# Giving the gate/up weights' buffers three places of their own, 32, 96 and 160 bytes (modulo 256) behind those of the rows, and the small buffers 224

## The chip, the cores and the metric

The kernel runs on one core of one Trainium2 chip. The metric is device time in microseconds (us) of one execution, as the median of several runs. TensorE is called PE, its weight loads PEld, VectorE DVE, ScalarE ACT, GpSimd POOL, and SyncE, which issues the DMA transfers, SP.

## What is computed

Two layers of a decoder trunk over 512 positions of width 1024, in float32. A layer mixes tokens in three ways at once (spatial gating, retention, forgetting attention), projects the result back, then runs a gated MLP with a short causal convolution, and adds a gated embedding. The part that the change is about is the MLP:

```python
def conv_gated_mlp(h, w_gate, w_up, conv_w, conv_b, w_down):   # D_FF = 4096
    g = h @ w_gate                                   # 512 x 1024 by 1024 x 4096
    gp = jnp.pad(g, ((0, 0), (CONV_WIDTH - 1, 0), (0, 0)))
    conv = conv_b + gp[:, 0:S] * conv_w[0]
    for j in range(1, CONV_WIDTH):
        conv = conv + gp[:, j:j + S] * conv_w[j]
    act = jax.nn.gelu(conv, approximate=True) * (h @ w_up)
    return act @ w_down                              # 512 x 4096 by 4096 x 1024

    h = rmsnorm(x, ffn_pre_g[i])
    x = x + rmsnorm(conv_gated_mlp(h, ...), ffn_post_g[i])
    gate = jax.nn.sigmoid(rmsnorm(x, ple_pre_g[i]) @ w_ple_gate[i])
    e = p[i] @ w_ple_proj[i]
    x = x + rmsnorm(e * gate, ple_post_g[i])
```

## The kernel before

**Precision.** Each float32 operand of a large product is split into a high part in TensorE's fp32r format and the remainder: `split` (L629) lets ACT copy the high part and DVE subtract it from the source. A product of two split operands takes three matmuls (high by high, high by low, low by high; `mm3`, L786).

**Gate and up together.** The MLP (`ffn`, L1120) treats w_gate and w_up in 32 blocks of 128 columns. `gate_up` (L1137) computes both products of a block in the manner of a fast matrix multiplication: the 512 positions and the 1024 features are halved, and seven products of 128 x 512 weights with 512 x 256 rows take the place of eight. The seven sums of the rows (hb11, hb21, hh6, hd, hh7, hb22, hh4) are made once per layer. The sums of the weights are made per block: the raw weights come in a tile `graw` (1 MB, two DMAs of 512 KB), `wg` and `wu` are split from it, then DVE adds parts of it to one another in place (four additions of 128x512), then `wsa` is split from the first half and `wsb` from the second. `product` (L1132) runs 12 matmuls of 128x128 weights (stationary) by 256 columns of the rows (moving). The products in order are two of wg, two of wsa, two of wsb and one of wu, 84 matmuls, for each of 32 blocks in each of two layers: 768 matmuls per product in all. They gather in two PSUM banks, `beta` and `ag`. Between the first product of wsa and those before it ACT must copy `beta` to `gs`, since wsa's product goes on adding to the same bank. So PE waits for that copy unless it has other work.

**Down.** After `wsb` of a block come pieces of the down product of the four blocks before (`pieces`, L1209; `down`): matmuls of 512 columns into `dn`, from `act` (the split activations, stationary) and `thl` (split weights, moving). The product of wu stands between the first 22 and the last 2 of such a piece.

**What sets the order.** Nothing in this code runs directly. The class `Plan` (L51) records every operation; `issue` (L247) simulates the engines with modelled costs and emits the operations in the order of that simulation, for each engine. An operation may start in the model only when its tiles have slots. All tiles of 8 KB per partition share one tag, "b8", with 24 slots of which every one belongs to a set, `SETS`. A tile of a named kind may take a slot of its own set only; a tile without a kind (raw weights, x, the embedding's `e`, gains, sums) takes a slot of the set with most room left (`pick`, L307). The kinds are given by `b8` (L545): W for wg, wsa and wsb; X for every other tile of type fp32r, among them the rows, `act` and `thl`. The `wu` tiles are of 2 KB and lie with `gs`, `us`, `cv` and other small tiles in the pool `kp`.

**Where the buffers lie.** The pools are opened one after another (L525 to L531): the set X, a pad, the set W, then `kp`. The pad is a tile of 16 floats per partition. Since the slots are of 8192 bytes and the base of X is a multiple of 256, every X slot lies at 0 modulo 256, and every W slot and every tile of `kp` at 64.

**The start of an MLP.** Before block 0 PE computes the embedding product (`embed`, L1285): its results, two tiles `e`, are copied from PSUM by ACT and DVE and stored to DRAM through SP, and the tiles are in use until those stores have landed. The first two blocks' weights are split at the same time.

Of the kernel before, what the change touches and what calls it, by code (L numbers as in the profile page):

```python
# [28 lines left out]
F32 = mybir.dt.float32  # L29
F32R = mybir.dt.float32r  # L30
# [6 lines left out]
P = 128  # L37
# [13 lines left out]
class Plan:  # L51
# [5 lines left out]

    SETS = {"X": 18, "W": 6}  # L60

    AHEAD = {"mix": 460, "wo": 230, "wo2": 230, "emb": 185, "gu0": 720, "gu": 460, "dn": 245, "end": 770, "pg": 450, "pg2": 120}
    LOAD = 1290
# [48 lines left out]
    def sets(self, pools):  # L112

        def tile_(shape, dt, name, kind):
            key = f"t{len(self.tiles)}"

            def make():
                c, i = self.place[key]
                return pools[c].tile(shape, dt, tag=f"{c}{i}", name=name, bufs=1)
            self.tiles[key] = ["b8", sum(self.SETS.values()), [], False, make, dt]  # L120
            self.kind[key] = kind
# [125 lines left out]
    def issue(self):  # L247
# [17 lines left out]
        for t in first:  # L265
            tag, bufs = self.tiles[t][0], self.tiles[t][1]
            slots.setdefault(tag, [0.0] * bufs)
            live.setdefault(tag, np.zeros(n + 1, np.int16))[first[t]:last[t] + 1] += 1
        unused = {c: [(0.0, i) for i in range(k)] for c, k in self.SETS.items()}
        inside = {c: np.zeros(n + 1, np.int16) for c in self.SETS}  # L270
        for t, c in self.kind.items():
# [12 lines left out]
        then, kind = None, "T"  # L284
        parked = {tag: [] for tag in (*slots, *(f"b8 {k}" for k in (*self.SETS, None)))}
        taken = {}
# [20 lines left out]
        def pick(t):  # L307

            if self.kind[t] is not None:
                c, s = self.kind[t], first[t]  # L310
                return c if unused[c] and (s <= front or inside[c][front:s].max() < self.SETS[c]) else None
            room = [(self.SETS[c] - inside[c][front:last[t] + 1].max(), c) for c in self.SETS if unused[c]]
            spare, c = max(room, default=(0, None))
# [204 lines left out]
def body(ctx, tc, a, out):  # L518
    nc = tc.nc
    plan = Plan(tc)  # L520
    V, A, G, T, SY = (plan.engine(n, e) for n, e in (
        ("DVE", nc.vector), ("ACT", nc.scalar), ("POOL", nc.gpsimd), ("PE", nc.tensor), ("SP", nc.sync)))
# [2 lines left out]
    large = {}  # L525
    for i, c in enumerate(Plan.SETS):
        large[c] = ctx.enter_context(tc.tile_pool(name="b" + c, bufs=1))
        if i + 1 < len(Plan.SETS):
            pad = ctx.enter_context(tc.tile_pool(name=f"pad{i}", bufs=1)).tile([P, 16], F32, tag="pad", name="pad", bufs=1)
            nc.gpsimd.memset(pad, 0.0)  # L530
    kp = ctx.enter_context(tc.tile_pool(name="kp", bufs=1))  # L531
    wp = ctx.enter_context(tc.tile_pool(name="wp", bufs=1))
    pp = ctx.enter_context(tc.tile_pool(name="pp", bufs=8, space=bass.MemoryType.PSUM))
# [9 lines left out]
        return kpt(list(shape), dt, tag="wk", name=name, bufs=12)  # L543

    def b8(name, shape, dt=F32):  # L545
        kind = "W" if name in ("wg", "wsa", "wsb") else "X" if dt == F32R else None
        return b8t([P] + list(shape), dt, name, kind)

    def small(name, n, dt=F32, bufs=4):
# [13 lines left out]
    class Rows:  # L563
# [3 lines left out]
        def load(self, c, queue=SY):  # L567
            if self.t[c // 2] is None:
                self.t[c // 2] = b8("x", (2, D))
            queue.dma_start(out=self[c], in_=self.src[:, c, :])  # L570
# [7 lines left out]
    class Gains:  # L578
# [5 lines left out]
        def __getitem__(self, at):  # L584
            if self.t is None:
                self.t = b8("gain", (2, D))
                for i, src in enumerate(self.src):
                    if src is not None:
                        name, l = src
                        SY.dma_start(out=self.t[:, i, :], in_=a[name][l:l + 1, :].to_broadcast([P, D]))  # L590
            return self.t[at]
# [56 lines left out]
    class Plain:  # L648
# [6 lines left out]
        def __call__(self, c, x):  # L655
            if self.t is None:
                self.t = [[b8("hT", (4, S), F32R) for _ in range(2)] for _ in range(2)]
                self.rs = small("rs", NCH)
            for kh in range(2):
                cs = slice(kh * 512, kh * 512 + 512)  # L660
                h = wk("h")
                V.tensor_tensor(out=h, in0=x[:, cs], in1=self.g[:, 1, cs], op=ALU.mult)
                pv = v4(transposed(h))
                ts = slice(c * P, c * P + P)
                split(self.t[0][kh][:, :, ts], self.t[1][kh][:, :, ts], pv)
# [730 lines left out]
```

## Time and profile before

| | before |
|---|---|
| runs | 1590.88, 1589.14, 1589.31 us |
| median of the runs | 1589.31 us |
| the profiled execution | 1587.76 us |
| its span in the trace | 1585.7 us |
| PE busy | 1559.8 us (98%), 10034 matmuls |
| DVE busy | 1233.2 us (78%) |
| ACT busy | 837.2 us (53%) |
| DMA | 197.47 MB, mean 125 GB/s |

The span is that part of the profiled execution in which instructions run. Busy time is a sum over an engine's instructions. In the rows of groups, the first number after the bar is busy time and the second the mean duration of one instruction; a matmul starts before the one ahead of it has ended, so the time from start to start (called the pitch here) is shorter than a duration. In a timeline's row stand the start in the span, the duration of the whole row, the engine, the line, the instruction with output and inputs, and, in brackets, a wait ahead of it and its releaser. All recorded operations carry the line of the helper, L444, so instructions are told apart by their tiles.

### The profile page before, as it was taken

The page shows a single profiled execution, that of the slowest core. Times are in us where ns is not written, and L with a number is a line of the kernel's source. Part 1 is how long each engine was busy: PE and PEld are TensorE (multiplying, and loading weights), DVE is VectorE, ACT ScalarE, POOL GpSimd, SP SyncE. Part 2 cuts the span into 40 slices and gives each one's busy share as a digit, 9 for nine tenths or more (in the row PEclk, how much of TensorE's full clock was granted, in tenths as well). Part 3 has the DMA queues.
Part 4 walks back from the last instruction along what each step waited for, and adds up shares of the span by engine and source line. Part 5 has one row for each costly group of instructions (what it writes and reads, how often), then busy time and mean ns, then how long its engine had stood idle before and what let it go on. Part 6 is the DMA issues. An engine that isn't in the chain of part 4 may idle for free.

```text
span 1585.7 us, 25202 instructions
## 1 busy us (share of the span) xinstructions
PE 1559.8 (98%) x10034; PEld 1388.1 (88%) x10034; DVE 1233.2 (78%) x2013; ACT 837.2 (53%) x1380; POOL 91.3 (6%) x157
## 2 busy tenths in 40 slices
PE   7999998999999999999999999989999999999998
PEld 6887787999999999998888777889999999999987
DVE  6556869988878888878664658699887897898785
ACT  7324637665555555554552446477655555555453
POOL 1100020000000000002220000200000000000021
PEclk9999999999999999999999999999999999999999
DMA  8113147223323422424463023362332233234433
GB/s 316 68 55 107 61 168 265 81 80 115 125 81 103 137 80 88 153 100 180 179 250 107 28 80 116 125 252 81 108 116 97 92 123 106 83 131 134 148 141 124
DMA packets 63421, 197.47 MB, mean 125 GB/s; under 512 B 7348, under 2 KB 15164, under 8 KB 63304
## 3 DMA queue, kind: packets, MB, share of 16 engines
q1 hardware_dynamic: 63160, 195.81, 35.1%
q8 instruction: 78, 1.28, 0.3%
q14 instruction: 39, 0.32, 0.1%
q10 hardware_dynamic: 144, 0.07, 0.0%
HBM read 178.52 MB, written 17.33 MB: 124 GB/s over the span
## 4 chain that ended last, share of the span: by engine, by line
PE 95%; DVE 2%; DMA 1%; ACT 1%; POOL 0%; issue 0%; SPq 0%; POOLq 0%; DVEq 0%; ACTq 0%
PE beta L444 22%; PE dn L444 22%; PE ag L444 16%; PE ps L444 15%; PE rps L444 4%; PE fps L444 4%; PE gps L444 2%; PE wo L444 2%; PE sps L444 1%; PE hps L444 1%; PE tps L444 1%; PE ops L444 1%; PE rops L444 1%; DMA graw<-in_w_gu_dram 1%; PE ips L444 0%
## 5 line engine op out<-in xcount | busy, mean ns | idle before, releaser
L444 PE MATMUL dn<-thl,act 128*128 128x512 f32 x1536 | 371.4, 391 | 0.0
L444 PEld LDWEIGHTS dn<-thl,act 128*128 128x128 f32 x1536 | 279.9, 188 | 51.9
L444 PE MATMUL ps<-thl,hT 128*128 128x512 f32 (+3 forms) x984 | 207.1, 368 | 0.1
L444 PEld LDWEIGHTS ps<-thl,hT 128*128 128x128 f32 x984 | 177.0, 189 | 23.3 <-DVE thl L444 1.2
L444 DVE TENSOR_TENSOR graw<-graw 128x512 f32<-128x512 f32 x256 | 169.2, 684 | 1.0
L444 DVE TENSOR_TENSOR thl<-traw,thl 128x1024 fp32r<-128x1024 f32 (+2 forms) x120 | 140.4, 1184 | 13.6 <-ACT thl L444 13.6
L444 ACT CAST thl<-traw 128x1024 fp32r<-128x1024 f32 (+2 forms) x120 | 120.1, 1018 | 9.0 <-DMA traw<-in_w_pg_dram 4.6
L444 PE MATMUL beta<-hh,wsa 128*128 128x256 f32 x768 | 101.4, 281 | 7.8 <-ACT gs L444 7.5
L444 PEld LDWEIGHTS beta<-hh,wsa 128*128 128x128 f32 x768 | 94.7, 192 | 8.7 <-ACT gs L444 7.9
L444 PEld LDWEIGHTS beta<-hb,wg 128*128 128x128 f32 x768 | 97.7, 189 | 4.9
L444 PEld LDWEIGHTS beta<-hh,wu 128*128 128x128 f32 x768 | 98.2, 189 | 4.2
L444 PE MATMUL beta<-hh,wu 128*128 128x256 f32 x768 | 100.4, 280 | 0.0
L444 PE MATMUL beta<-hb,wg 128*128 128x256 f32 x768 | 99.9, 278 | 0.0
L444 PE MATMUL ag<-hb,wg 128*128 128x256 f32 x768 | 98.6, 276 | 0.0
L444 PE MATMUL ag<-hd,wsa 128*128 128x256 f32 x768 | 98.5, 278 | 0.0
L444 PE MATMUL beta<-hh,wsb 128*128 128x256 f32 x768 | 98.4, 276 | 0.0
L444 DVE SCALAR_TENSOR_TENSOR cv<-gs,cw,cv 128x511 f32<-128x511 f32 (+1 forms) x128 | 95.1, 743 | 3.6 <-ACT cv L444 3.5
L444 PE MATMUL ag<-hb,wsb 128*128 128x256 f32 x768 | 97.9, 276 | 0.0
L444 ACT ACTIVATE cv<-gs,cw 128x512 f32<-128x512 f32 x64 | 52.2, 816 | 82.4 <-DVE gs L444 82.4
L444 ACT COPY gs<-beta 128x256 f32<-128x256 f32 x128 | 47.2, 371 | 88.4 <-PE beta L444 86.6
L444 DVE TENSOR_TENSOR wsb<-graw,wsb 128x1024 fp32r<-128x1024 f32 x64 | 78.0, 1219 | 19.8 <-ACT wsb L444 15.0
L444 PEld LDWEIGHTS ag<-hd,wsa 128*128 128x128 f32 x768 | 93.1, 190 | 0.0
(193 smaller groups left out, 2655.7 us busy)
## 6 DMA issues: line engine op xcount, KB each, us to landing
graw<-in_w_gu_dram SPq DMA_DIRECT2D x128, 512.0 KB, 6.2
traw<-in_w_dn_dram SPq DMA_DIRECT2D x64, 512.0 KB, 5.0
x<-x SPq DMA_DIRECT2D x40, 512.0 KB, 5.0
fraw<-in_w_fm_dram SPq DMA_DIRECT2D x30, 512.0 KB, 8.8
traw<-in_w_wo_dram SPq DMA_DIRECT2D x16, 512.0 KB, 4.2
traw<-in_w_pg_dram SPq DMA_DIRECT2D x16, 512.0 KB, 8.6
x<-in_x_dram SPq DMA_DIRECT2D x8, 512.0 KB
traw<-in_w_uv_dram SPq DMA_DIRECT2D x8, 512.0 KB, 8.1
```

Of the source, the lines that this page charges most:

```text
L444: made = o[1](*[self.map(v) for v in o[2]], **{k: self.map(v) for k, v in o[3].items()})
```

## The change

The set W of six slots becomes three sets of two: G for wg, A for wsa, B for wsb. The pad behind X is 8 floats (32 bytes) in place of 16, and a pad of 16 floats follows every later set, the last one too. So wg lies at 32 modulo 256, wsa at 96, wsb at 160, and `kp`, with wu in it, at 224. X stays at 0. The number of 8 KB slots is 24 as before.

```diff
-    SETS = {"X": 18, "W": 6}
+    SETS = {"X": 18, "G": 2, "A": 2, "B": 2}
...
     for i, c in enumerate(Plan.SETS):
         large[c] = ctx.enter_context(tc.tile_pool(name="b" + c, bufs=1))
-        if i + 1 < len(Plan.SETS):
-            pad = ctx.enter_context(tc.tile_pool(name=f"pad{i}", bufs=1)).tile([P, 16], F32, tag="pad", name="pad", bufs=1)
-            nc.gpsimd.memset(pad, 0.0)
+        n = 8 if i == 0 else 16
+        pad = ctx.enter_context(tc.tile_pool(name=f"pad{i}", bufs=1)).tile([P, n], F32, tag="pad", name="pad", bufs=1)
+        nc.gpsimd.memset(pad, 0.0)
...
-        kind = "W" if name in ("wg", "wsa", "wsb") else "X" if dt == F32R else None
+        kind = {"wg": "G", "wsa": "A", "wsb": "B"}.get(name, "X" if dt == F32R else None)
```

The smaller sets also change what the planner finds free, and so the order of some instructions. On PE, where the first layer's MLP starts (hb and hh are sums of the rows), before:

```order
L444 MATMUL beta<-hb_2163,wg 128x256 x12
L444 MATMUL ag<-hb_2175,wg 128x256 x12
L444 MATMUL beta<-hh_2258,wsa 128x256 x2
L444 MATMUL beta<-hb_2163,wg 128x256 x5
L444 MATMUL beta<-hh_2258,wsa 128x256 x10
L444 MATMUL ag<-hd,wsa 128x256 x12
L444 MATMUL beta<-hh_2266,wsb 128x256 x2
```

The same place on PE after:

```order
L444 MATMUL beta<-hb_2184,wg 128x256 x12
L444 MATMUL ag<-hb_2196,wg 128x256 x12
L444 MATMUL beta<-hb_2184,wg 128x256 x12
L444 MATMUL ag<-hb_2196,wg 128x256 x12
L444 MATMUL beta<-hh_2279,wsa 128x256 x2
L444 MATMUL ag<-hd,wsa 128x256 x2
L444 MATMUL beta<-hh_2279,wsa 128x256 x10
L444 MATMUL ag<-hd,wsa 128x256 x10
```

Both products of block 1's wg now stand ahead of the first wsa. On ACT at the same place (COPY e is the end of the embedding, COPY gs the copy that frees beta), before:

```order
L444 CAST wu<-graw 128x512
L444 COPY e<-eps 128x512
L444 CAST wsa<-graw 128x1024
L444 COPY gs<-beta 128x256
L444 CAST wg<-graw 128x1024
L444 CAST wu<-graw 128x512
L444 CAST wsb<-graw 128x1024
L444 COPY gs<-beta 128x256
```

The same place on ACT after:

```order
L444 CAST wu<-graw 128x512
L444 COPY e<-eps 128x512
L444 COPY gs<-beta 128x256
L444 CAST wsb<-graw 128x1024
L444 CAST wu<-graw 128x512
L444 COPY gs<-beta 128x256
L444 CAST wsb<-graw 128x1024
L444 CAST wsa<-graw 128x1024
L444 CAST wu<-graw 128x512
L444 CAST wsa<-graw 128x1024
```

The copy gs has moved ahead of every cast, and the first wsa behind both casts of wsb. In the steady part of the MLP the order on PE reads the same in both, but for the numbers in the tiles' names.

## The prediction

> **What bounds the kernel now.** I read the busy times first, then the chain that ended last.
>
> ```profile
> span 1585.7 us, 25202 instructions
> PE 1559.8 (98%) x10034; PEld 1388.1 (88%) x10034; DVE 1233.2 (78%) x2013; ACT 837.2 (53%) x1380; POOL 91.3 (6%) x157
> PE 95%; DVE 2%; DMA 1%; ACT 1%; POOL 0%; issue 0%; SPq 0%; POOLq 0%; DVEq 0%; ACTq 0%
> ```
>
> TensorE is busy 98% of the span and is 95% of the chain, so only two things can move the end: the time from one matmul to the next, and PE's few waits. The change touches addresses, which could alter the first, and the slots that the planner hands out, which could alter the second. The windows after the start of the first layer's FFN show where there is nothing to wait for (columns: us; busy of PE, PEld, DVE, ACT, POOL; granted clock; DMA share; GB/s):
>
> ```profile
> 258.00:272.00 14.00, 9.93 (x67) 9.27 (x66) 14.00 (x21) 8.85 (x15) 0.00 (x0) 0.88 1.03 410
> 302.00:704.00 402.00, 402.00 (x2897) 376.62 (x2897) 337.05 (x479) 218.48 (x336) 0.00 (x0) 1.00 0.31 105
> 1042.00:1057.00 15.00, 11.24 (x72) 10.90 (x71) 14.42 (x21) 9.27 (x15) 0.00 (x0) 0.77 1.03 413
> ```
>
> From 302 to 704 us PE never pauses, at a granted clock of 1.00. PE is idle at the two FFN starts, 4.07 us of 14.00 and 3.76 us of 15.00, with the clock down to 0.88 and 0.77 as a mean.
>
> Now the matmuls themselves. A block of gate/up is seven products of 12 matmuls over 256 columns; weights are stationary, the rows' sums (set X) are moving. One block in steady state, in the timeline of PE (start, duration of the whole group, instruction, count):
>
> ```profile
> 529.12 1.53 PE L444 MATMUL beta<-hb,wg 128*128 128x256 f32 x12
> 530.48 1.52 PE L444 MATMUL ag<-hb,wg 128*128 128x256 f32 x12
> 531.84 1.52 PE L444 MATMUL beta<-hh,wsa 128*128 128x256 f32 x12
> 533.20 1.52 PE L444 MATMUL ag<-hd,wsa 128*128 128x256 f32 x12
> ...
> 537.28 5.17 PE L444 MATMUL dn<-thl,act 128*128 128x512 f32 x22
> 542.29 1.58 PE L444 MATMUL beta<-hh,wu 128*128 128x256 f32 x12
> 543.71 0.63 PE L444 MATMUL dn<-thl,act 128*128 128x512 f32 x2
> 544.17 1.53 PE L444 MATMUL beta<-hb,wg 128*128 128x256 f32 x12
> ```
>
> The start of one group to the next gives the pitch: 1.36 us / 12 = 113.3 ns for wg and wsa, 1.42 / 12 = 118.3 for wu, 5.01 / 22 = 227.7 for dn, which is 113.9 per 256 columns. In the built program every X slot lies at 0 modulo 256; wg, wsa, wsb and wu all lie at 64. In dn both operands are X, offset 0.
>
> The same thing by groups (busy us, mean ns of one), with one more product of two X operands, this time over 256 columns:
>
> ```profile
> L444 PE MATMUL beta<-hh,wsb 128*128 128x256 f32 x768 | 98.4, 276 | 0.0
> L444 PE MATMUL beta<-hh,wu 128*128 128x256 f32 x768 | 100.4, 280 | 0.0
> L444 PE MATMUL ps<-thl,hT 128*128 128x256 f32 x48 | 5.9, 283 | 0.0
> ```
>
> A matmul of 276 ns goes with a pitch of 113.3, so a duration holds 163 ns beside its pitch; 283 ns means a pitch of about 120 and wu's mean 280 about 117. So for 256 columns offset 0 costs 120 and offset 64 costs 113.3, in short phases 118. That is the trace's whole evidence that the offset matters at all.
>
> **Part 1: the pads.** One pad of 64 bytes becomes four (32, 64, 64, 64), with three more memsets on POOL, busy 6% of the span: nothing. The moves are: wg from 64 to 32, wsa to 96, wsb to 160, wu to 224. Per block the counts are 24, 24, 24 and 12 matmuls, over 64 blocks 1536, 1536, 1536 and 768.
>
> No row shows an offset of 32, 96, 160 or 224, so I bound the pitch from both sides. At full clock 256 columns can hardly go below half of what a half-clocked matmul takes. In the second layer's start a window at granted clock 0.50 holds 15 matmuls:
>
> ```profile
> 1051.00:1054.00 3.00, 3.00 (x15) 3.00 (x15) 3.00 (x5) 1.01 (x2) 0.00 (x0) 0.50 1.03 416
> ```
>
> Fifteen matmuls touch 3.00 us without a pause, the first and the last in part: 14 pitches, 214 ns each, and half of that at full clock is about 107 (an estimate). Best case: the 4608 matmuls of wg, wsa and wsb go from 113.3 to 106.8 or so: −30 us. Worst case: they go to the 118.3 of wu's row, 5.0 × 4608 = +23 us, or to the 120 of offset 0, 6.7 × 4608 = +31 us. wu alone, from 118.3 to 113.3 at best and 120 at worst: −3.8 to +1.3 us.
>
> I take no change. The nearest rows are the two that are already quoted: 113.3 at offset 64 over 256 columns and 113.9 per 256 at offset 0 over 512. Two quite different placements stop at the same time per column, which looks like a floor that placement doesn't set; 64 is already on it. A straight line from offset 0 (120) to 64 (113.3) would give wg 116.7 at 32, +3.4 × 1536 = +5 us, and I keep that inside the range.
>
> The page "TensorE: Matmul & The Clock Gate" of the Trainium skill, section "Back-to-back issue gap", has N/2.4 + 2.5 ns from one matmul to the next: as an estimate 109.2 for 256 columns and 215.7 for 512. This trace shows 113.3 and 227.7, so here the excess grows with the columns and is not a fixed gap. If the change brought the page's figure, 4.1 ns × 5376 matmuls would be −22 us; that is one of the rivals.
>
> **Part 2: the slots.** A set W of six becomes three of two, and each of wg, wsa, wsb may only take its own. In steady state the order of PE is unchanged (the same product sequence), and PE had no stall there. At the FFN's start it is another matter. PE and ACT before:
>
> ```profile
> 260.33 1.58 PE L444 MATMUL ag<-hb,wg 128*128 128x256 f32 x12
> 265.68 0.51 PE L444 MATMUL beta<-hh,wsa 128*128 128x256 f32 x2 [3.77 <-ACT gs L444]
> 267.27 2.50 PE L444 MATMUL beta<-hh,wsa 128*128 128x256 f32 x10 [0.29 <-DVE wsa L444]
> 269.57 1.68 PE L444 MATMUL ag<-hd,wsa 128*128 128x256 f32 x12
> 262.02 0.58 ACT L444 COPY e<-eps 128x512 f32<-128x512 f32 x1
> 264.31 1.04 ACT L444 CAST wsa<-graw 128x1024 fp32r<-128x1024 f32 x1 [1.71 <-DVE graw L444]
> 265.26 0.36 ACT L444 COPY gs<-beta 128x256 f32<-128x256 f32 x1
> ```
>
> PE has done wg by 261.75 and waits 3.77 us, since ACT makes wsa (264.31) ahead of the copy gs that frees beta. Then the clock is halved: ten matmuls of wsa take 2.30 us (267.27 to 269.57) instead of 1.13.
>
> In the changed order ACT does gs right after e and wsa only four casts later; PE does block 1's wg in the gap. Why so late: the built program gives set A's two slots to block 0's raw weights and to an e tile, and wsa can be written only when one is free. The raw tile is in use until wsb and wsa themselves are read from it, so it is the e tile that has to go, and it goes when its stores have landed:
>
> ```profile
> 258.88 4.06 SPq L444 DMA_DIRECT2D e<-e  x3
> DMA to landing us min/median/max: 2.0/8.0/8.7
> ```
>
> The last of them is issued at about 262.9 and lands 8 us on, near 271. Before, wsa stood in a slot whose user was done long ago. DVE and ACT have work enough until then:
>
> ```profile
> 260.65 1.22 DVE L444 TENSOR_TENSOR wg<-graw,wg 128x1024 fp32r<-128x1024 f32 x1
> 262.99 0.68 DVE L444 TENSOR_TENSOR wu<-graw,wu 128x512 fp32r<-128x512 f32 x1
> 263.59 2.49 DVE L444 TENSOR_TENSOR graw<-graw 128x512 f32<-128x512 f32 x4
> 266.00 1.22 DVE L444 TENSOR_TENSOR wsa<-graw,wsa 128x1024 fp32r<-128x1024 f32 x1
> 267.13 0.42 DVE L444 TENSOR_TENSOR gs<-ag,gs 128x256 f32<-128x256 f32 x1
> 267.47 0.68 DVE L444 TENSOR_TENSOR graw<-graw 128x512 f32<-128x512 f32 x1
> ```
>
> By starts, wu and one graw take 0.60 each (262.99 to 263.59; 2.41 / 4), wsa or wsb 1.13, gs 0.34. In the changed order DVE has, between graw x4 (done at 266.0) and wsa, two of each: wu, graw, wsb, gs, 5.3 us, so it is busy to 271.3 without wsa. PE does 24 more matmuls of wg (ready at 261.9; 24 × 0.113 = 2.7 us, to 264.7) and then has nothing until wsa's high part, written from 271 to 272 (1.04 by its row): 7.3 us idle. Then 0.3 for the low part, as before, and the half clock. What that costs is in the window's row of before: 0.12 × 14.00 = 1.7 us beside 4.07 of idle, 5.8 in all. After: 7.3 + 0.3 + 1.7 = 9.3. Difference **+3.5 us**. Bounds: +2, if the last store lands in 6.5 us, and +6, if it takes the row's 8.7 and the half clock lasts a microsecond or two longer for the longer rest. PE has no later pause in which to win it back.
>
> In layer 2 wsa's slot is free sooner, and its start moves less: ACT does wsa and wsb ahead of gs, one cast of 1.04 us more, but PE takes some wg matmuls into that gap. I put **+1 us** (0 to +1.5).
>
> **The sum.** 0 for the pitch, +3.5 and +1 for the starts: +4.5 us. The profiled execution took 1587.76 us (its span of 1585.7 and 2.1 around it), so 1592.3 on its scale; the median of the runs is 1.55 above it, 1589.31, so the forecast is **1594 us**.
>
> **The rivals.**
>
> *A better pitch.* If the 6.7 ns from 120 to 113.3 is a clash of two reads that shrinks as operands lie further apart, then 96 and 160 may bring another half of it: −3.3 × 3072 = −10 us, with wg unchanged and wu at 113.3 (−3.8): −14, with the starts −9.5, so 1580 us; if only wsa and wsb gain, 1584. It decides as soon as the pitch falls by 1 ns (−4.6 us). For it: 120 against 113.3, wu's phases. Against it: 113.3 and 113.9 at two offsets and column counts. I give 0.22.
>
> *No clash left at all.* If 113.3 itself still holds a clash that any of the four new offsets avoids, all 5376 matmuls of gate/up go half way to the 107 of the half-clock window or further: −3.2 × 5376 = −17 us, with the starts −12.5: 1577 us; the whole way, 1559. The 113.9 of dn speaks against it as above, and dn itself would gain nothing, its operands staying at 0. Chance 0.08. With the page's 109.2 for the new pitch it would be −22 + 4.5, or 1572 us.
>
> *A worse pitch.* Today wg, wsa and wsb share one offset and the stream of weights never changes phase within six products; wu's 118.3 behind dn (offset 0 to 64) looks like what a change of offset costs. With four offsets each boundary is such a change: 5.0 × 4608 = +23 us at worst, half of it (+12) if only some products are hit: 1606 to 1617 us. For it: wu's row stands exactly behind a change of operands. Against it: wg follows dn too, at 544.17, and runs at 113.3. Chance 0.24.
>
> *The starts cost nothing.* If the e stores land 3 us sooner, wsa goes where it was and the pitch is unchanged: 1589.3 us, the time of before. For it: the row's minimum of 2.0 us. Against it: its median of 8.0. Chance 0.04.
>
> *The change does nothing by address.* The page "SBUF — State Buffer" of the Trainium skill, section "Who interferes with whom", says that only DVE and GpSimd contend for a port, and that PE never waits on another engine. By that no offset alters a matmul's pitch, and what is left is my sum of +4.5. The row of 283 ns against 276 speaks against it, though more than the place of the operands differs there. It gives the forecast's own time and shares its chance of 0.42; a change of pitch in any group of 768 would refute it.
>
> **How the numbers follow.** 0.2% is 3.2 us, about what a measurement of this kernel can tell from no change. The forecast (0.42) spreads from +2 to +7.5 and is slower by over 3.2 us in three cases of four: 0.32 slower, 0.10 same. The worse pitch adds 0.24 slower. The two better ones are faster with 0.25, and with 0.05 the gain is just eaten by the starts: same. The last 0.04 is the same. Together 0.25 faster, 0.19 same, 0.56 slower. The range leaves out about one in ten on each side: below, no clash left at all beyond the half way of 1577, hence 1575; above, all of the worse pitch with the starts but its end, hence 1615. The forecast's own range is 1591 to 1597.
>
> **What would show it.** Right: groups of wg, wsa, wsb with means of 276 to 281 ns as before, and in the changed profile a wait of PE of 6 to 8 us before the first wsa near 265 us, put down to ACT's wsa. Wrong: means of 273 or less, or of 283 and more, in the groups of 768; a PE wait under 4 us at the first FFN start. A mean of 273 in wsb's group alone would already be −2.3 us for each product.

## The result and the profile after

The changed kernel takes 1626.93 us (median of four runs, 1625.72 to 1628.51), beside 1589.22 for the kernel before: 1.0236 times as long, with a 95% interval of 1.0218 to 1.0254. That is 37.7 us slower. The forecast was 1594, the range 1575 to 1615: the sign came as forecast, the size did not, by a factor of eight.

The head of the profile after and its chain:

```profile
span 1623.0 us, 25172 instructions
PE 1589.3 (98%) x10034; PEld 1413.9 (87%) x10034; DVE 1237.1 (76%) x2013; ACT 839.2 (52%) x1380; POOL 89.0 (5%) x160
PE 93%; DVE 3%; DMA 1%; ACT 1%; issue 1%; POOL 1%; SPq 0%; POOLq 0%; DVEq 0%; ACTq 0%
```

The span grew by 37.3 us. PE's busy time grew by 29.5 with the same 10034 matmuls, so most of the loss is in the matmuls themselves; the other 8 are idle time. By groups (busy us, mean ns of one):

```profile
L444 PE MATMUL beta<-hb,wg 128*128 128x256 f32 x768 | 102.6, 281 | 0.0
L444 PE MATMUL beta<-hh,wsa 128*128 128x256 f32 x768 | 105.8, 288 | 11.9 <-ACT wsa L444 6.7 <-ACT gs L444 4.5 <-DVE wsa L444 0.7
L444 PE MATMUL beta<-hh,wsb 128*128 128x256 f32 x768 | 102.1, 282 | 0.8 <-ACT gs L444 0.8
L444 PE MATMUL beta<-hh,wu 128*128 128x256 f32 x768 | 100.1, 279 | 0.1
```

wsb went from 276 to 282 ns, wu from 280 to 279. A block in steady state shows the pitch without the waits and the half-clock stretches that stand in these means (timeline of PE after; start, duration of the group, count):

```profile
525.80 1.56 PE L444 MATMUL beta<-hh,wu 128*128 128x256 f32 x12
527.20 0.62 PE L444 MATMUL dn<-thl,act 128*128 128x512 f32 x2
527.66 1.58 PE L444 MATMUL beta<-hb,wg 128*128 128x256 f32 x12
529.08 1.58 PE L444 MATMUL ag<-hb,wg 128*128 128x256 f32 x12
530.49 1.60 PE L444 MATMUL beta<-hh,wsa 128*128 128x256 f32 x12
531.93 1.60 PE L444 MATMUL ag<-hd,wsa 128*128 128x256 f32 x12
533.38 1.59 PE L444 MATMUL beta<-hh,wsb 128*128 128x256 f32 x12
534.80 1.60 PE L444 MATMUL ag<-hb,wsb 128*128 128x256 f32 x12
536.24 5.20 PE L444 MATMUL dn<-thl,act 128*128 128x512 f32 x22
541.28 1.56 PE L444 MATMUL beta<-hh,wu 128*128 128x256 f32 x12
```

From start to start: wg 1.42 / 12 = 118.3 ns, wsa 1.44 / 12 = 120.0, wsb 118.3 and 120.0, wu 1.40 / 12 = 116.7. Only wu got faster. The whole block takes 15.48 us from one wu to the next (525.80 to 541.28); before, it took 15.05 from one wg to the next (529.12 to 544.17).

The start of the first layer's MLP, PE and then ACT, after:

```profile
264.97 1.57 PE L444 MATMUL ag<-hb,wg 128*128 128x256 f32 x12
273.23 0.80 PE L444 MATMUL beta<-hh,wsa 128*128 128x256 f32 x2 [6.69 <-ACT wsa L444]
271.19 1.04 ACT L444 CAST wsb<-graw 128x1024 fp32r<-128x1024 f32 x1 [2.08 <-DVE graw L444]
272.14 1.04 ACT L444 CAST wsa<-graw 128x1024 fp32r<-128x1024 f32 x1
```

PE waits 6.69 us for wsa, in place of 3.77 us for the copy gs. The size of the wait is as forecast. In these rows ACT waits for graw ahead of wsb, and wsa follows without a wait of its own: no wait for the landing of e's stores shows here, and what makes wsa late is its place in the order.

Where the time comes in can be read by following the same matmul through the timelines of two kernels. The table has its start before and how much later it comes in four others (us; the last three are experiments that are told below). Each column is one execution, and executions of the kernel before lie up to 4.9 us apart (1587.03 to 1591.92), so a difference of a microsecond or two between columns says little:

| matmul | before | after | order alone | e kept out | three slots each |
|---|---|---|---|---|---|
| first wg, layer 1 | 258.9 | +1.8 | +2.0 | +2.6 | +5.0 |
| first wsb of block 4, layer 1 | 308.7 | +7.9 | +8.0 | +8.4 | +7.8 |
| last dn, layer 1 | 748.3 | +19.8 | +10.0 | +10.0 | +11.6 |
| first wg, layer 2 | 1042.5 | +20.2 | +10.5 | +11.6 | +13.3 |
| first wsb of block 4, layer 2 | 1092.9 | +25.1 | +14.5 | +15.1 | +14.9 |
| end | 1585.7 | +37.3 | +16.5 | +17.0 | +18.9 |

### The profile page after: what moved, and what is told of

Read it like the earlier page. It is cut to its first block, busy times and chain, and to the rows that moved or that the text cites. A ratio compares the mean times of both kernels' runs of the same rounds, so it can differ in the third digit from the quotient of the medians.

```text
span 1623.0 us, 25172 instructions
## 1 busy us (share of the span) xinstructions
PE 1589.3 (98%) x10034; PEld 1413.9 (87%) x10034; DVE 1237.1 (76%) x2013; ACT 839.2 (52%) x1380; POOL 89.0 (5%) x160
## 4 chain that ended last, share of the span: by engine, by line
PE 93%; DVE 3%; DMA 1%; ACT 1%; issue 1%; POOL 1%; SPq 0%; POOLq 0%; DVEq 0%; ACTq 0%
PE beta L444 22%; PE dn L444 21%; PE ag L444 16%; PE ps L444 15%; PE rps L444 4%; PE fps L444 4%; PE gps L444 2%; PE wo L444 2%; PE hps L444 1%; PE sps L444 1%; PE tps L444 1%; PE ops L444 1%; PE rops L444 1%; DMA e<-e 1%; DVE thl L444 0%
## 5 line engine op out<-in xcount | busy, mean ns | idle before, releaser
L444 DVE TENSOR_TENSOR graw<-graw 128x512 f32<-128x512 f32 x256 | 175.2, 687 | 2.0
L444 ACT CAST thl<-traw 128x1024 fp32r<-128x1024 f32 (+2 forms) x120 | 120.1, 1019 | 6.1 <-DMA traw<-in_w_pg_dram 3.4
L444 ACT CAST wsb<-graw 128x1024 fp32r<-128x1024 f32 x64 | 67.1, 1049 | 106.5 <-PE ag L444 100.9
L444 PE MATMUL beta<-hh,wsa 128*128 128x256 f32 x768 | 105.8, 288 | 11.9 <-ACT wsa L444 6.7
L444 PEld LDWEIGHTS beta<-hh,wsa 128*128 128x128 f32 x768 | 99.0, 195 | 13.0 <-ACT wsa L444 6.9
L444 PE MATMUL ag<-hd,wsa 128*128 128x256 f32 x768 | 104.1, 285 | 1.2 <-DVE gs L444 1.2
L444 PE MATMUL beta<-hh,wsb 128*128 128x256 f32 x768 | 102.1, 282 | 0.8 <-ACT gs L444 0.8
L444 PE MATMUL ag<-hb,wsb 128*128 128x256 f32 x768 | 102.4, 282 | 0.0
L444 PEld LDWEIGHTS ag<-hd,wsa 128*128 128x128 f32 x768 | 98.1, 193 | 1.5 <-DVE gs L444 1.4
L444 PEld LDWEIGHTS beta<-hh,wsb 128*128 128x128 f32 x768 | 96.0, 189 | 1.2 <-ACT gs L444 1.0
```

The costliest lines, as they stand in the source:

```text
L444: made = o[1](*[self.map(v) for v in o[2]], **{k: self.map(v) for k, v in o[3].items()})
```

## The experiments

Theory A, formed on these numbers: the place of a weight relative to the rows (its distance modulo 256) sets its pitch, and the smaller sets cost some waits beside. Theory B: it is the change of distance from one product to the next that costs. Theory C: the sets and the new order are the whole loss. In the experiments the pads come from a tuple, the number of floats behind each set in turn; the times of before beside them are 1588.5 to 1589.3.

**Order alone.** The three sets as in the changed kernel, with everything at 64:

```diff
     SETS = {"X": 18, "G": 2, "A": 2, "B": 2}
...
+    pads = (16, 0, 0, 0)
     for i, c in enumerate(Plan.SETS):
         large[c] = ctx.enter_context(tc.tile_pool(name="b" + c, bufs=1))
-        n = 8 if i == 0 else 16
-        pad = ctx.enter_context(tc.tile_pool(name=f"pad{i}", bufs=1)).tile([P, n], F32, tag="pad", name="pad", bufs=1)
-        nc.gpsimd.memset(pad, 0.0)
+        if pads[i]:
+            pad = ctx.enter_context(tc.tile_pool(name=f"pad{i}", bufs=1)).tile([P, pads[i]], F32, tag="pad", name="pad", bufs=1)
+            nc.gpsimd.memset(pad, 0.0)
```

> The three sets and so the changed order, but no pads between the sets: wg, wsa, wsb and wu all lie at 64 modulo 256 as before. Order alone. Theory A (the distance of a weight from the rows sets its pitch, the order costs only the waits where the MLPs start): pitch 113.3 ns, +10 us, about 1599. Theory C (the smaller sets are the whole loss): about 1627.

Measured: 1603.87 us, a ratio of 1.0090 (1.0073 to 1.0106). One group is enough to show the pitch:

```profile
L444 PE MATMUL ag<-hb,wg 128*128 128x256 f32 x768 | 98.4, 276 | 0.0
```

It is the 276 ns of before. So C falls, and the sets with their order are worth about 15 us, more than the 10 expected. Since the changed kernel has the same sets and order, the rest, over 20 us, is its offsets.

**One set, other places.** The kernel before, its one set of six and its order untouched, and only the pad behind X changed; a second pad keeps the small buffers at 64.

```diff
     SETS = {"X": 18, "W": 6}
-    pads = (16, 0)     # W at 64
+    pads = (8, 8)      # W at 32; second run (24, 56), W at 96; third (40, 40), W at 160
```

> The one set of six of before, and its order, moved from 64 to 32 modulo 256; the small buffers stay at 64. Theory A (each distance has its own pitch): all three weights at the 117 ns that wg shows in the changed kernel, +3.7 x 4608 = +17 us, about 1606. Theory B (it is the change of distance from one product to the next that costs): 113.3 ns, about 1589.

> The one set of six at 96 modulo 256, small buffers at 64. Theory A: all three weights at wsa's 120 ns, +6.7 x 4608 = +31 us, about 1620. Theory B: 113.3 ns, about 1589.

> The one set of six at 160 modulo 256, small buffers at 64. Theory A: all three weights at the 119.7 ns of wsb, +6.4 x 4608 = +29 us, about 1618. Theory B: 113.3 ns, about 1589.

Measured: 1610.15 at 32 (1.0130, 1.0115 to 1.0145), 1604.89 at 96 (1.0100, 1.0085 to 1.0115), 1616.77 at 160 (1.0175, 1.0160 to 1.0190). Two rows of the steady timeline of PE, at 32:

```profile
522.16 1.58 PE L444 MATMUL ag<-hb,wg 128*128 128x256 f32 x12
523.58 1.59 PE L444 MATMUL beta<-hh,wsa 128*128 128x256 f32 x12
```

At 96:

```profile
521.17 1.57 PE L444 MATMUL ag<-hb,wg 128*128 128x256 f32 x12
522.58 1.57 PE L444 MATMUL beta<-hh,wsa 128*128 128x256 f32 x12
```

At 160:

```profile
523.79 1.60 PE L444 MATMUL ag<-hb,wg 128*128 128x256 f32 x12
525.23 1.60 PE L444 MATMUL beta<-hh,wsa 128*128 128x256 f32 x12
```

The pitch is 1.42 / 12 = 118.3 ns at 32, 1.41 / 12 = 117.5 at 96, 1.44 / 12 = 120.0 at 160. Here no distance changes between wg, wsa and wsb, and the instructions stand in the order of before: B falls as the main cause, and A holds in the main. The rise over 113.3 times the 4608 matmuls would be 23, 19 and 31 us, near the measured 21.7, 16.4 and 28.3. It missed one thing: 96 gives 117.5 here and not the 120 that wsa has at 96 in the changed kernel. Ahead of the first down product of layer 1, the same run has 120 as well:

```profile
307.93 1.60 PE L444 MATMUL beta<-hh,wsa 128*128 128x256 f32 x12
309.37 1.60 PE L444 MATMUL ag<-hd,wsa 128*128 128x256 f32 x12
```

That is 1.44 / 12 = 120.0, with wg and wsb at 120.0 beside it; behind the down product that follows, all three are at 117.5. So one distance can have two pitches.

**What a product follows.** The changed kernel with wg moved from 32 to 96, so that wsa follows its like:

```diff
-    pads = (8, 16, 16, 16)   # wg 32, wsa 96, wsb 160, wu 224
+    pads = (24, 0, 16, 16)   # wg 96, wsa 96, wsb 160, wu 224
```

> The changed kernel with wg moved from 32 to 96, so that wsa (96) follows a product of its own distance; wsb stays at 160, wu at 224. In the changed kernel wsa ran at 120.1 ns, in the one set at 96 at 117.4. If a product's pitch also depends on the one ahead of it: wsa 117.4 in both its products, wg 117.4: -2.7 x 1536 - 0.8 x 1536 = -5 us, about 1622. If it is the order or the sets that made wsa slower: wsa stays at 120, about 1626.

Measured: 1622.05 us, 1.0214 (1.0199 to 1.0229), by medians 4.9 us under the changed kernel. The timeline of PE:

```profile
533.04 1.57 PE L444 MATMUL beta<-hh,wsa 128*128 128x256 f32 x12
534.45 1.57 PE L444 MATMUL ag<-hd,wsa 128*128 128x256 f32 x12
535.85 1.60 PE L444 MATMUL beta<-hh,wsb 128*128 128x256 f32 x12
```

wsa takes 117.5 ns and 1.40 / 12 = 116.7; its buffers and its order are those of the changed kernel, and only what goes ahead of it is different. So in steady state wsa's pitch depends on what goes ahead of it too, by 2.5 to 3 ns: a small part of B is true. A change of distance just ahead is not needed for the slower pitch, as the first blocks of the run with one set at 96 have shown: what goes ahead seems to choose between the two pitches of 96. The time agrees with the 5 us expected, though the intervals of the two ratios overlap; from the first wsb of block 4 to the last dn in layer 1, and from there to the end in layer 2, its trace takes 2.5 and 2.7 us less than that of the changed kernel.

**Farther places.** The one set at 128 and at 192:

```diff
-    pads = (16, 0)     # W at 64
+    pads = (32, 48)    # W at 128; second run (48, 32), W at 192
```

> The one set of six of before at 128 modulo 256, small buffers at 64. So far, with one set: 32 gave 118.2 ns, 64 113.3, 96 117.4, 160 119.8; two products of rows at distance 0 ran at 120. Theory A1 (the distance counts modulo 128, so 160 reads as 32 and 128 as 0): about 120 ns, +6.7 x 4608 = +31 us, 1619. Theory A2 (the distance counts modulo 256 and the farthest place is the best): 113.3 ns or less, 1588 or less.

> The one set of six at 192 modulo 256, small buffers at 64. Both A1 (192 reads as 64) and a symmetry about 0 (192 is 64 in front of the rows): 113.3 ns, about 1588. If neither holds (the lower half is simply better than the upper one): 119 to 120 ns, about 1617.

Measured: 1611.73 at 128 (1.0146, 1.0131 to 1.0161), 1606.30 at 192 (1.0115, 1.0099 to 1.0132). The steady timeline of PE at 128:

```profile
522.27 1.59 PE L444 MATMUL ag<-hb,wg 128*128 128x256 f32 x12
523.70 1.58 PE L444 MATMUL beta<-hh,wsa 128*128 128x256 f32 x12
```

It is 1.43 / 12 = 119.2 ns, and 118.7 as the median of its groups, near the 120 that a count modulo 128 would give. At 192 two states appear, before and behind the first down product of layer 1:

```profile
307.14 1.52 PE L444 MATMUL ag<-hd,wsa 128*128 128x256 f32 x12
308.50 1.52 PE L444 MATMUL beta<-hh,wsb 128*128 128x256 f32 x12
...
311.22 5.17 PE L444 MATMUL dn<-thl,act 128*128 128x512 f32 x22
...
535.22 1.57 PE L444 MATMUL ag<-hb,wg 128*128 128x256 f32 x12
536.63 1.57 PE L444 MATMUL beta<-hh,wsa 128*128 128x256 f32 x12
```

In layer 1 it is 113.3 ns up to the first dn, 117.5 to 118 from then on. In layer 2 it starts at 117.8, falls to 113.3 before the first dn (from about 1089 us on) and is 117.8 behind it again. Neither rule that I had held: 192 doesn't read as 64, and 160 (120.0) doesn't read as 32 (118.3). The distance 192 can have the good pitch and doesn't keep it; in the kernel before, 64 has it for wg, wsa and wsb behind every down product.

**Distance or place.** The kernel before with all of it, rows included, moved up by 32 bytes:

```diff
     large = {}
+    first = ctx.enter_context(tc.tile_pool(name="first", bufs=1)).tile([P, 8], F32, tag="first", name="first", bufs=1)
+    nc.gpsimd.memset(first, 0.0)
     pads = (16, 0)     # X now at 32, W and the small buffers at 96
```

> The kernel before with everything behind a new pad of 32 bytes: rows, act and thl at 32, wg, wsa, wsb and wu at 96 modulo 256, the distance still 64. If it is the distance from the rows that counts: 113.3 ns for the three weights, 118 for most of wu, about 1588.5. If it is the place of the weights itself: 117.4 ns as with the one set at 96, +4.1 x 4608 = +19 us or what the rows' own place adds, about 1605 or more.

Measured: 1588.69 us, 0.9996 (0.9986 to 1.0005). Steady timeline of PE:

```profile
532.64 1.52 PE L444 MATMUL ag<-hb,wg 128*128 128x256 f32 x12
534.00 1.52 PE L444 MATMUL beta<-hh,wsa 128*128 128x256 f32 x12
```

1.36 / 12 = 113.3 ns, with the weights at 96, where they took 117.5 beside rows at 0. In steady state it is the distance between the two operands that counts, as far as this one move shows. In the first four blocks of both layers it is otherwise:

```profile
299.41 1.58 PE L444 MATMUL ag<-hd,wsa 128*128 128x256 f32 x12
300.82 1.58 PE L444 MATMUL beta<-hh,wsb 128*128 128x256 f32 x12
```

That is 1.41 / 12 = 117.5 ns, where the kernel before has 113.3 at the same distance. The run on order alone, with rows at 0 and weights at 64, has 117.8 in the first blocks of layer 1 too, and 113.3 in those of layer 2. So 64 has two pitches as well, and the new place can't be the whole reason for the slower one. The profiled execution was the slowest of its ten (1590.81 us); whether the others had the slower pitch there isn't known.

**The small buffers.** The kernel before with the second pad alone, so that wu lies at 224, then at 192:

```diff
-    pads = (16, 0)     # small buffers at 64
+    pads = (16, 40)    # at 224; second run (16, 32), at 192
```

> The kernel before with the small buffers alone at 224 modulo 256; wg, wsa, wsb stay at 64. Theory A: wu at 116.7 ns as in the changed kernel, in place of 113 to 118: -0.8 us, about 1588. If the small buffers' place matters to what else they hold (gs, us, cv): several us slower, with the weights still at 113.3 ns.

> The kernel before with the small buffers alone at 192. At 192 the three weights ran at 113.3 ns in the first four blocks of a layer and at 117.8 after the first down product. wu stands behind a down product in 52 of 64 blocks. If the state is set by what the product follows: wu at 118 in those blocks as at 64, about 1588.5. If a change of place can avoid it: 113.3, -2.9 us, about 1585.6.

Measured: 1588.03 us at 224 (0.9998, 0.9989 to 1.0007) and 1588.87 at 192 (1.0001, 0.9992 to 1.0010), no change that can be told. wu's group of 768 in the run at 224:

```profile
L444 PE MATMUL beta<-hh,wu 128*128 128x256 f32 x768 | 100.0, 279 | 0.0
```

279 in place of 280 ns: the gain of 1 ns per matmul came as expected, 0.8 us in all. At 192 wu ran at 117 to 120 ns in 56 of 64 blocks. None of the three places tried, 64, 192 and 224, gave wu the good pitch behind a down product.

**What the sets cost.** First, the embedding's tiles kept out of the small sets:

```diff
-        kind = {"wg": "G", "wsa": "A", "wsb": "B"}.get(name, "X" if dt == F32R else None)
+        kind = {"wg": "G", "wsa": "A", "wsb": "B"}.get(name, "X" if dt == F32R or name == "e" else None)
     pads = (16, 0, 0, 0)
```

> The three sets of two, all at 64, as in the run on order alone (1603.9 us), but the embedding's tiles e may only take slots of set X. If e's stores held set A's slot at the first MLP start: PE's 6.9 us ahead of the first wsa shrink to the 3.9 of before, -3 us, about 1600; the waits in blocks 2 to 4 of each layer stay. If the raw weights or DVE's order of work held wsa: 1604.

Measured: 1604.13 us, 1.0097 (1.0083 to 1.0111): nothing gained. The timeline of PE at the first start:

```profile
262.88 1.58 PE L444 MATMUL ag<-hb,wg 128*128 128x256 f32 x12
270.13 2.93 PE L444 MATMUL beta<-hh,wsa 128*128 128x256 f32 x12 [5.67 <-ACT gs L444]
```

wsa went back to its old place in the order, ahead of gs, and comes 3.3 us sooner than in the run on order alone. But at block 4 both kernels are 8 us behind (the table above): what was won at the start was lost again. So the slots that e took did decide the order there (that it was the landing of its stores, no run shows), and yet were not what the time hung on.

Then three slots each, 15 for the rest:

```diff
-    SETS = {"X": 18, "G": 2, "A": 2, "B": 2}
+    SETS = {"X": 15, "G": 3, "A": 3, "B": 3}
     pads = (16, 0, 0, 0)
```

> All at 64 modulo 256 as in the run on order alone, but with three slots for each of wg, wsa, wsb and 15 in place of 18 for the rest. If two slots are too few for sets that the raw weights also use: most of the +15 us goes, 1590 to 1594. If the loss comes from keeping the names apart at all: about 1604. If X is short with 15: new waits on thl, act or hT, above 1600 with the matmuls at 113.3 ns.

Measured: 1606.36 us, 1.0108 (1.0092 to 1.0123). The table divides it: from the first wg to block 4 it loses 2.8 us in layer 1 and 1.6 in layer 2, where two slots each lose 6.1 and 4.0. The third slot gave back over half; in layer 1 a part of that may be pitch, since the run with two slots was at 117.8 ns in those blocks and this one at 113.3. But it is 3 us later at the first wg already. X is three slots short, but that this is the reason isn't shown: the changed kernel with wg at 96, whose X has 18 slots, is 4.4 us behind the kernel before at that place in its profiled execution. And from block 4 to the end of the layer it loses 3.9 us in layer 1 and 4.0 in layer 2, where two slots lose 2.0 and 2.0. So none of the single answers held.

Windows of the first blocks of layer 1 show how PE and DVE stand. Before (columns: us; busy of PE, PEld, DVE, ACT, POOL; clock; DMA share; GB/s):

```profile
269.00:284.00 15.00, 15.00 (x130) 15.00 (x130) 13.98 (x22) 9.67 (x16) 0.00 (x0) 0.97 0.56 229
284.00:299.00 15.00, 15.00 (x135) 15.00 (x134) 15.00 (x24) 9.32 (x16) 0.00 (x0) 1.00 0.27 86
299.00:309.00 10.00, 10.00 (x90) 10.00 (x89) 10.00 (x14) 9.70 (x17) 0.00 (x0) 1.00 0.23 83
```

Order alone:

```profile
271.00:286.00 15.00, 12.34 (x87) 12.04 (x88) 13.30 (x18) 8.81 (x12) 0.00 (x0) 0.77 0.58 230
286.00:301.00 15.00, 15.00 (x130) 15.00 (x129) 11.30 (x19) 10.38 (x17) 0.00 (x0) 1.00 0.18 62
301.00:317.00 16.00, 15.18 (x127) 14.86 (x126) 16.00 (x23) 10.91 (x19) 0.00 (x0) 1.00 0.40 132
```

In the kernel before PE is never idle here and DVE 1.0 us of 40: both are full, and PE lives on what DVE has prepared. In the run on order alone DVE is idle 1.7 + 3.7 us of 30, after which it is busy 16.00 of 16.00 while PE loses 0.82. Layer 2 doesn't repeat this. The run on order alone there:

```profile
1063.00:1078.00 15.00, 15.00 (x121) 15.00 (x120) 12.93 (x19) 9.79 (x16) 0.00 (x0) 0.89 0.55 224
1078.00:1093.00 15.00, 15.00 (x135) 15.00 (x133) 14.93 (x24) 10.35 (x17) 0.00 (x0) 1.00 0.34 90
```

DVE is busy 12.93 and 14.93 us, hardly less than in the kernel before at that place (13.31 and 15.00), and yet 4.0 us are lost up to block 4. So DVE's idle time can't be the whole reason. The groups show what the casts wait for, ACT's cast of wsb before and then in the run on order alone:

```profile
L444 ACT CAST wsb<-graw 128x1024 fp32r<-128x1024 f32 x64 | 67.2, 1051 | 21.0 <-PE ag L444 19.8 <-DVE graw L444 1.2
```

```profile
L444 ACT CAST wsb<-graw 128x1024 fp32r<-128x1024 f32 x64 | 67.1, 1048 | 99.3 <-PE ag L444 93.6 <-DVE graw L444 5.6
```

With two slots of its own, wsb's cast waits for PE to finish a product, 93.6 us over the run in place of 19.8. In steady state that costs little: from block 4 to the last dn of layer 1 the run on order alone falls only 2.0 us further back. Nor does this wait alone measure the loss: with three slots it is still 76.2 us, while the first blocks lose less than half. That the run on order alone loses 6.1 and 4.0 us in the first blocks of the two layers is measured (in layer 1 with whatever the slower pitch there adds); through which waits they do it stays open.

## Why the prediction was wrong

- **"I take no change" for the pitch: wrong, and it is the step that failed.** It held 113.3 to be "a floor that placement doesn't set; 64 is already on it". As a floor it stood: no gate/up product's median in any run was below 113.3. But that 64 lies on the floor says nothing of 32, 96 or 160. The row of dn, 113.9 per 256 columns at distance 0, was called the nearest and was not: it has 512 columns. The row of the same shape at another distance was quoted beside it, 283 ns or 120 at distance 0, and it gave about the right size. Measured: +4.9 for wg, +6.8 for wsa, +6.4 for wsb (medians of the groups: about 118.2, 120.1, 119.7), times 1536 each, and −1 × 768 for wu: 27 us, inside the bounds of −30 and +31 that stood there.
- **The straight line** (116.7 at 32, kept for the range) was wrong by 1.5 ns; between 0, 32, 64, 96, 128, 160 and 192 the pitch goes 120, 118.3, 113.3, 117.5, 118.7, 120, 118 and follows no line.
- **The worse pitch as a rival** (chance 0.24) was the case that came, 5.0 × 4608 = +23 us, but for a reason that is mostly wrong. It put the cost on changes of distance between products; the runs with one set have none between wg, wsa and wsb and are as slow. Only wsa's last 2.5 to 3 ns go with what stands ahead. Its own times, 1606 to 1617, were 10 us short even so: the pitch took 4 us more than its +23, and the sets 6 more than the 4.5 of the starts.
- **The better pitch, and no clash left** (0.30 together): no place tried gave it. The page "TensorE: Matmul & The Clock Gate" of the Trainium skill would have had 109.2 ns, as an estimate; no run came near it, since the best of gate/up was 113.3.
- **The change does nothing by address:** refuted, as its condition said. The rule quoted there from the page "SBUF — State Buffer" of the Trainium skill, that PE never waits on another engine, speaks of engines. What was measured is a matmul's rate following the distance between its own two operands, with 28 us between the places 64 and 160.
- **The starts:** +3.5 and +1 forecast. From the first wg to the first wsa of block 1 the changed kernel fell back by 3.6 us in layer 1 and 0.9 in layer 2, and PE's wait was 6.69 us where 7.3 idle was worked out. Up to there the size was right, the reason half right: e's slots did decide the order, but with e kept out of them the same time was lost by block 4.
- **"PE has no later pause"** was used to say that the loss at the start stays. It also took the later blocks to be free of loss. There PE ran without a pause beside a DVE that was idle 1.0 us of 40, and that left little room. The sum put the sets at 4.5 us, all of it at the two starts. They cost 1.8 us ahead of the first MLP and more in the blocks up to 4, so that about 10 us of the changed kernel's 37.7 are theirs. Alone they cost 15; that slower matmuls cover a part of the waits is argued, not shown.
- **The bands of the last part** were too wide to be a test: "276 to 281 ns as before" spans 113 to 118 ns of pitch, so wg's 281 would have passed as no change while it cost 7.5 us. Of its signs, PE's wait of 6.69 us spoke for the forecast, and wsa's mean of 288 against it.

## What to carry to other kernels

Where two operands of a matmul lie relative to each other was worth up to 1.75% of a kernel in which TensorE is busy 98% of the span. It has to be measured place by place, with order and sets held still; a row of the same shape at another distance is the best price to be had, and a row of another shape is none. When a pool is split by names, look at the first blocks, where the engine that prepares has little time to spare: of the 16.5 us that the run on order alone is behind in its trace, 10.1 fell there and 4.0 in all the later blocks.

## What the runs showed of the hardware

- In steady state the pitch of 256-column matmuls depends on the distance modulo 256 between stationary and moving operand: 113.3 ns at 64, 117 to 120 at 32, 96, 128, 160 and 192. Moving both operands by 32 bytes left the steady pitch at 113.3 and the time at 1588.69 us.
- It has a memory, and several distances have two pitches: 64 and 192 have 113.3 and 118, 96 has 117.5 and 120. In layer 1, 192 went from 113.3 to 118 and 96 from 120 to 117.5 at the first 512-column product at distance 0. Behind such products wg at 64 was at 113.3 in the kernel before and wu, at 64 too, at 118. What carries that state is open: the runs show when it changes, not why.
- At half clock the distance cost nothing that shows. In stretches at a granted clock of 0.50 (268 to 269 us before and with the one set at 160, 275 to 277 us after) a matmul of wsa took 213 to 214 ns from start to start at each of the distances 64, 160 and 96.
